# Four small experts in 64 slots, as plain fp32 matmuls in column pairs, in an order sorted on the chip

## The chip, the cores and the metric
The kernel runs on one core of a Trainium2 chip. Times are device microseconds of one launch, from the launch to the last instruction's end. The core's engines are PE (matmuls; PEld is its weight loads), DVE, ACT, POOL and SP, whose queue issues nearly all DMA transfers.

## What is computed
A two-layer trunk on 256 tokens of 1024 channels. The change lies in its last part, a mixture of experts: the router picks two of eight experts for a token, and an expert is a SwiGLU with 2816 hidden channels.

```
logits = xf @ router_w + router_b
top_vals, top_idx = lax.top_k(logits, 2)
gates = softmax(top_vals)
combine = sum(one_hot(top_idx, 8) * gates[..., None], axis=1)
for e in range(8):
    ye = (silu(xf @ w1[e]) * (xf @ w3[e])) @ w2[e]
    out = out + combine[:, e:e + 1] * ye
```

Ahead of it stand an RMSNorm, attention, pooling, a dense SwiGLU and a state-space mixer; behind it a residual and the final RMSNorm. All arrays are fp32.

## The kernel before
Only an expert's own tokens are computed. The router's logits become one-hots and ranks (a token's slot within its expert), and `Rows` (L1093) gathers the rows of an expert with matmuls of the tokens by a token-to-slot one-hot `P` of 128 slots. `scatter` (L1150) brings the outputs back with the transposed one-hot `PT`. Should an expert have over 128 tokens, a branch at the end (L1284) runs it again for the rest.

The weights are packed into tiles of 128 x 2048 fp32 (1 MB). An expert has 11 blocks (`NBLK`) of 256 hidden channels, and a block three tiles: two (A) of w1 beside w3, one (B) of w2. `load` (L87) takes a tile from a ring of 11 buffers (`raw`: 3 and `NR2` = 8) and issues its DMA on SP's queue. So the 264 tiles of the experts are issued in the order of use, each as soon as its buffer is free.

A product of fp32 values is made of three fp32r matmuls: `split` (L105) makes `hi` (a cast, ACT, L116) and `lo` (a subtraction, DVE, L117) of each half of a tile, in a ring of seven half tiles (`hi`: 6 and `NH2` = 1), and `mm3` (L120) multiplies hi by hi, hi by lo and lo by hi (L121 to L123). The rows are split likewise (`gx`, L1138 and L1140).

For each block `experts` (L1222) issues ffn_in (24 matmuls of 128 slots by 512 columns into a bank `p`), then ffn_out of the block before (12 matmuls into two banks `y`), then `ffn_T`: two transposes of the gated product `g` (Silu on ACT, L489, a multiply on DVE, L490), whose result is split into `th` and `tl` (L504). Two experts share one gather; experts run in the order 0 to 7. Engines run their own instructions in order. That order comes from a scheduler, which also moves instructions between the lines of the program.

Of the kernel before, what the change touches and what calls it, by code (L numbers as in the profile page):

```python
# [15 lines left out]
D = 1024  # L16
# [10 lines left out]
NR2, NH2 = 8, 1  # L27


# tiles of the packed weights, by number  # L30
# [6 lines left out]
def trunk_kernel(tc, x, par, cb, w_pool, wt, we, final_norm, out):  # L37
# [17 lines left out]
    with es:  # L55
# [38 lines left out]
        class Halves:  # L94
            """a tile of 2048 columns in two halves"""
# [29 lines left out]
        # -------------------------------------------------------- constants  # L125
# [3 lines left out]
        # small parameters: gains, forget bias, S5 scalars, forget and router weights  # L129
# [21 lines left out]
        def keep_clock(n, *behind):  # L151
            """short matmuls that keep the tensor engine's clock up over a wait"""
# [8 lines left out]
        def rms(src, junk):  # L161
            """returns 1 / rms, and the last instructions on ACT, DVE and Pool"""
# [44 lines left out]
        # S5 discretisation: a e^{dt} in polar form  # L207
# [23 lines left out]
        # ============================================================ mixer 0  # L231
        with ExitStack() as e0:
# [4 lines left out]
            # forget-gate selectors: row r = 32 i + h  # L237
# [14 lines left out]
            # causal mask of a diagonal block, four heads wide  # L252
# [6 lines left out]
            # 1 / min(t + 1, window)  # L259
# [12 lines left out]
            # ---- norm, transposed activations  # L272
# [14 lines left out]
            # ---- projections, channels on partitions  # L287
# [18 lines left out]
            # log sigmoid(z) = min(z, 0) - ln(1 + exp(-|z|))  # L306
# [24 lines left out]
            # ---- pooling branch  # L331
# [21 lines left out]
            # ---- q (scaled, one head per slot, the other head's rows zero), k, v  # L353
# [28 lines left out]
            # pooled map  # L382
# [15 lines left out]
            # ---- attention  # L398
# [125 lines left out]
        # ------------------------------------------------- complex helpers  # L524
# [63 lines left out]
                        # masks of the two groups of a pair, by state row and by channel row  # L588
# [14 lines left out]
                        # (abar - 1) / a  # L603
# [30 lines left out]
                        # e^{i 4 theta 2^k}  # L634
# [15 lines left out]
                            # Re(C a^tau) and -Im(C a^tau)  # L650
# [57 lines left out]
                    # chunk rotation e^{i 4 theta c}  # L708
# [69 lines left out]
        # ============================================================ mixer 1  # L778
# [80 lines left out]
        # ---- chunk inputs, chunk scan, outputs; four pairs at a time.  # L859
        # The gated projection of a block of channels follows its group.  # L860
# [68 lines left out]
        # ================================================================ MoE  # L929
# [25 lines left out]
        def route_T(tb, c0, n, i):  # L955
            """n blocks of 128 channels: sum of squares, transposed activations"""
# [71 lines left out]
        moe2 = pool("moe2", bufs=2)  # L1028
        gu[0] = pool("gu2")
# [28 lines left out]
        cmx = f6.tile([128, NE + 1], F32, name="cmx")  # L1058
        sc.copy(cmx[:, 0:NE], t[:, 16:24])
# [3 lines left out]
        cnts = rt.tile([128, NE + 1], I32, name="cnts")  # L1063

        def gates():
# [15 lines left out]
            ve.tensor_copy(cnts, cmx)  # L1081
# [283 lines left out]
```

## Time and profile before

| | us |
|---|---|
| runs | 1259.91, 1267.09, 1259.91 |
| median of the runs | 1259.91 |
| span of the profiled execution, first to last instruction | 1262.1 |
| PE busy in it | 1213.5 (96%) |
| DVE, ACT busy | 1084.0 (86%), 855.3 (68%) |

The runs' times do not say which of them was profiled; the span lies 2.2 above the median. Times in rows are us from the span's start, a mean or median of one instruction is in ns. A matmul's recorded duration overlaps with the next one's, so the distance of two starts, not the duration, says what a matmul costs.

### The profile page before, as it was taken

What the parts mean: (1) busy time and instruction counts of PE and PEld (TensorE: products, weight loads), DVE (VectorE), ACT (ScalarE), POOL (GpSimd) and SP (SyncE); (2) the same over time, 40 slices, a digit from 0 to 9 for tenths busy, and PEclk for the clock granted to TensorE, in tenths of its full rate; (3) what the DMA queues carried; (4) which work ended last, traced back from release to release, by engine and by line L of the source; (5) the groups of instructions that cost most, each with busy time, mean ns of one, the idle gap of its engine ahead of it and who ended that gap; (6) DMA issues with size and microseconds to landing.
All of it is one profiled execution on the core that took longest, in us unless ns stands there. A gap on an engine that the chain in (4) does not pass through costs nothing.

```text
span 1262.1 us, 16883 instructions
## 1 busy us (share of the span) xinstructions
PE 1213.5 (96%) x6188; PEld 998.6 (79%) x6189; DVE 1084.0 (86%) x1424; ACT 855.3 (68%) x1179; POOL 127.7 (10%) x132
## 2 busy tenths in 40 slices
PE   8998789999999999999999999999999999999995
PEld 8876568888878778888888888888888888888884
DVE  7776986688697779999999998899999999899996
ACT  6465336544475548888877877677777778777774
POOL 3303992000022110000000000000000000000000
PEclk9999789999999999999999999999999999999998
DMA  6524343543531658999998998998999997999960
GB/s 247 200 75 153 118 157 113 188 159 142 200 137 65 271 230 337 373 372 349 372 345 318 371 362 326 339 367 305 362 371 352 364 375 290 368 374 345 366 243 36
DMA packets 48138, 341.85 MB, mean 271 GB/s; under 512 B 5296, under 2 KB 5936, under 8 KB 6832
## 3 DMA queue, kind: packets, MB, share of 16 engines
q1 hardware_dynamic: 47904, 340.55, 71.7%
q8 instruction: 50, 0.82, 0.3%
q14 instruction: 40, 0.33, 0.1%
q10 hardware_dynamic: 144, 0.15, 0.0%
HBM read 339.63 MB, written 1.05 MB: 270 GB/s over the span
## 4 chain that ended last, share of the span: by engine, by line
PE 85%; DVE 9%; ACT 3%; issue 1%; POOL 1%; DMA 0%; ACTq 0%; DVEq 0%; POOLq 0%
PE p L122 16%; PE p L123 16%; PE p L121 15%; PE y L123 10%; PE y L121 10%; PE y L122 10%; DVE lo L117 3%; PE t L501 2%; PE t L1129 1%; PE t L687 1%; PE p L1129 1%; PE t L677 1%; ACT hi L116 1%; DVE ep L811 1%; PE t L874 0%
## 5 line engine op out<-in xcount | busy, mean ns | idle before, releaser
L117 DVE TENSOR_TENSOR lo<-raw,hi 128x1024 fp32r<-128x1024 f32 x642 | 777.1, 1244 | 91.1 <-ACT hi L116 77.1
L116 ACT CAST hi<-raw 128x1024 fp32r<-128x1024 f32 x642 | 650.0, 1050 | 123.1 <-PE y L123 46.7
L121 PE MATMUL p<-hi,gx 128*128 128x512 f32 x704 | 281.7, 401 | 0.0
L123 PE MATMUL p<-hi,gx 128*128 128x512 f32 x704 | 277.0, 393 | 0.0
L122 PE MATMUL p<-lo,gx 128*128 128x512 f32 x704 | 276.3, 393 | 0.0
L123 PE MATMUL y<-hi,tl 128*128 128x512 f32 x440 | 173.6, 395 | 3.1 <-DVE tl L504 3.1
L122 PE MATMUL y<-lo,th 128*128 128x512 f32 x440 | 172.8, 393 | 0.6 <-DVE lo L117 0.6
L121 PE MATMUL y<-hi,th 128*128 128x512 f32 x440 | 160.6, 393 | 0.2 <-ACT th L504 0.2
L122 PEld LDWEIGHTS p<-lo,gx 128*128 128x128 f32 x704 | 132.5, 188 | 30.0 <-DVE lo L117 1.1
L123 PEld LDWEIGHTS p<-hi,gx 128*128 128x128 f32 x704 | 132.2, 188 | 26.6
L121 PEld LDWEIGHTS p<-hi,gx 128*128 128x128 f32 x704 | 132.4, 188 | 25.4
L489 ACT ACTIVATE g<-p,rs 128x256 f32<-128x256 f32 x88 | 41.9, 476 | 86.7 <-PE p L123 86.6
L123 PEld LDWEIGHTS y<-hi,tl 128*128 128x128 f32 x440 | 83.1, 189 | 21.1 <-DVE tl L504 3.4
L122 PEld LDWEIGHTS y<-lo,th 128*128 128x128 f32 x440 | 82.9, 188 | 19.3 <-DVE lo L117 1.0
L121 PEld LDWEIGHTS y<-hi,th 128*128 128x128 f32 x440 | 83.1, 189 | 18.5 <-ACT th L504 0.5
L1187 POOL TENSOR_TENSOR fr<-fr,mhalf 128x1 f32<-128x1 f32 x2 | 1.5, 758 | 790.1 <-DVE fr L1185 790.1
L504 ACT CAST th<-t 128x256 fp32r<-128x256 f32 (+1 forms) x99 | 39.0, 394 | 56.3 <-PE t L501 56.3
L122 PE MATMUL p<-lo,h1h 128*128 128x512 f32 x176 | 71.6, 407 | 1.6 <-DVE lo L117 1.6
L121 PE MATMUL p<-hi,h1h 128*128 128x512 f32 x176 | 72.0, 410 | 0.0
L123 PE MATMUL p<-hi,h1l 128*128 128x512 f32 x176 | 70.8, 403 | 0.4 <-DVE h1l L204 0.4
L501 PE MATMUL t<-ident,g 128*128 128x128 f32 x220 | 41.1, 275 | 11.1 <-DVE g L490 11.1
L501 PEld LDWEIGHTS t<-ident,g 128*128 128x128 f32 x220 | 30.0, 141 | 25.3 <-DVE g L490 12.3
(382 smaller groups left out, 1455.8 us busy)
## 6 DMA issues: line engine op xcount, KB each, us to landing
raw<-in_we_dram SPq DMA_DIRECT2D x264, 1024.0 KB, 5.0
raw<-in_wt_dram SPq DMA_DIRECT2D x57, 1024.0 KB, 4.8
xt<-in_x_dram SPq DMA_DIRECT2D x2, 512.0 KB, 4.6
CB<-in_cb_dram SPq DMA_DIRECT2D x1, 1024.0 KB, 5.0
out_dram<-raw SPq DMA_DIRECT2D x4, 256.0 KB, 3.3
raw<-in_final_norm_dram SPq DMA_DIRECT2D x1, 512.0 KB, 4.2
wpl<-in_w_pool_dram SPq DMA_DIRECT2D x1, 256.0 KB, 9.1
pk<-in_par_dram ACTq DMA_DIRECT2D x1, 150.5 KB, 4.4
```

Source lines behind the costliest of these rows:

```text
L116: sc.copy(h.a[k][:, c], r[:, d])
L117: ve.tensor_sub(lo.a[k][:, c], r[:, d], f32(h.a[k][:, c]))
L121: pe.matmul(o, lh, rh, start=start, stop=False)
L122: pe.matmul(o, lh, rl, start=False, stop=False)
L123: pe.matmul(o, ll, rh, start=False, stop=stop)
L489: sc.activation(g1, p[:, 0:256], AF.Silu, scale=rs[:, tb:tb + 1])
L501: i0 = pe.transpose(v[:, f, tb * 128:(tb + 1) * 128], gs[tb][:, f * 128:(f + 1) * 128], ident)
L504: ffn_T.last = i0, sc.copy(th, v), ve.tensor_sub(tl, v, f32(th[:]))
L677: pe.transpose(t[:, k * 128:(k + 1) * 128], Vd[:, 2 * n2 + k // 2, k % 2].rearrange("p a b c -> p (a b c)"), ident)
L687: pe.matmul(t[0:32, k * 64:(k + 1) * 64], Bm[:, k, i].rearrange("p a b -> p (a b)"), Wu[:, c0 + k, i, 0:4].rearrange("p a b -> p (a b)"), ...
L811: ve.tensor_tensor_scan(ep[:, i], dv, ep[:, i], 0.0, op0=OP.mult, op1=OP.add)
L1129: pe.matmul(v, x_[:, tb, kc * 128:kc * 128 + 128], self.P[:, tb, 0:self.w], start=i + tb == 0, stop=i + tb == 2)
```

## The change
Expert 0 stays first, with 128 slots. Experts 1 to 7 are sorted by their number of tokens on the chip (`by_count`: 23 small DVE operations that also permute ranks and gates). The four with the fewest (positions 1 to 4, `NF` = 4) get 64 slots and take the new path; the other three stay as before. The order is 0, 1, 7, 2, 6, 3, 5, 4 by position, so large and small alternate. SP reads the expert's number into a register (`values_load`), and the DMA's address is made from it.

The new path does not split: `fast_in` multiplies 64 rows (stationary) by 256 columns of the raw tile in plain fp32, once for each half of the hidden channels, into the lower and the upper 64 partitions of one bank; `fast_out` does the same with the two halves of the output channels, 512 columns each. A branch still runs what does not fit into 64 or 128 slots. `raw` has 10 buffers instead of 11, `hi` six halves instead of seven. A large expert is gathered alone, all small ones together.

```diff
-NR2, NH2 = 8, 1
+NR2, NH2 = 7, 0
+NF = 4
...
+        order = [0]
+        for i in range(NE - 1):
+            order.append(i // 2 + 1 if i % 2 == 0 else NE - 1 - i // 2)
+
+        def room(p):
+            return 64 if 0 < p <= NF else 128
...
+        def by_count():
+            N = NE - 1
+            key = f6.tile([128, N], F32, name="key")
+            io1 = ioS[:, 1:NE]
+            ve.scalar_tensor_tensor(key, cmx[:, 1:NE], 8.0, io1, op0=OP.mult, op1=OP.add)
+            less = f6.tile([128, N, N], F32, name="less")
+            ve.tensor_tensor(less, key.unsqueeze(1).to_broadcast([128, N, N]),
+                             key.unsqueeze(2).to_broadcast([128, N, N]), op=OP.is_lt)
+            pos = f6.tile([128, N], F32, name="pos")
+            ve.tensor_reduce(pos, less, axis=AX.X, op=OP.add)
...
+            ve.tensor_copy(permi[:, 1:NE], num[:, 0, 1:NE])
+            for tb in range(2):
+                for s, d in ((rank[:, tb, 1:NE], rankp[:, tb, 1:NE]), (rg[:, tb, 2:], rgp[:, tb, 2:])):
+                    ve.tensor_tensor(tmp, sel, s.unsqueeze(1).to_broadcast([128, N, N]), op=OP.mult)
+                    ve.tensor_reduce(d, tmp, axis=AX.X, op=OP.add)
...
+        class Weights:
+            def __init__(self, p):
+                self.p = p
+                if p:
+                    self.r = nc.values_load(permi[0:1, p:p + 1], engines=[mybir.EngineType.SP], ...)
+            def load(self, i):
+                if self.p == 0:
+                    return load(we, i)
+                r = raw_tile()
+                nc.sync.dma_start(out=r, in_=we4[bass.ds(self.r, 1), i].rearrange("a p f -> (a p) f"))
+                return r
...
+        def fast_in(A, F, i):
+            p = ptile()
+            for s in range(2):
+                v = A[s].rearrange("p (k w f) -> p k w f", k=4, w=2)
+                for k in range(4):
+                    kc = 4 * s + k
+                    for h in range(2):
+                        pe.matmul(p[64 * h:64 * h + 64, 0:256].rearrange("p (w f) -> p w f", w=2),
+                                  F.x[:, kc, i * 64:i * 64 + 64], v[:, k, :, h * 128:h * 128 + 128],
+                                  start=kc == 0, stop=kc == 7)
+            g1 = gu[0].tile([128, 256], F32, name="g1", tag="g1")[:, 0:128]
+            sc.activation(g1, p[:, 0:128], AF.Silu, scale=F.rs[:, i, 0:1])
+            ve.scalar_tensor_tensor(g1, p[:, 128:256], F.rs[:, i, 1:2], g1, op0=OP.mult, op1=OP.mult)
+            return g1
+
+        def fast_T(g1):
+            t = ttile()
+            pe.transpose(t[:, 0:128], g1, ident)
+            h = gu[0].tile([128, 128], F32, name="hT", tag="hT", bufs=2)
+            sc.copy(h, t[:, 0:128])
+            return h
+
+        def fast_out(y, h, B, first, last):
+            for f in range(2):
+                for nb in range(2):
+                    c = f * D + nb * 512
+                    pe.matmul(y[64 * nb:64 * nb + 64], h[:, f * 64:f * 64 + 64], B[:, c:c + 512],
+                              start=first and f == 0, stop=last and f == 1)
...
+        def scatter_fast(P, y, acc, first, last):
+            t = ttile()
...
+            sc.copy(PT.rearrange("p a b -> p (a b)"), t[:, 0:256])
+            yf = tab.tile([128, 512], F32, name="yf", tag="t2")
+            sc.copy(yf[:, 0:256], y[:, 0:256])
+            ve.tensor_copy(yf[:, 256:512], y[:, 256:512])
+            o1 = [ttile(), ttile()]
+            for tb, os, i, j in ((0, acc, first, last), (1, o1, True, True)):
+                for nb in range(2):
+                    r = slice(64 * nb, 64 * nb + 64)
+                    pe.matmul(os[nb], PT[r, tb], yf[r], start=i, stop=j)
...
+                    gs = fast_in(A, F, p - 1) if fast else ffn_in(A, R.hi, R.lo, 1, R.rs[:, 0:1], R.rs[:, 1:2])
                     if prev is not None:
                         tail(prev)
                     if b == 0:
-                        ys = [[ytile(), ytile()]]
-                    prev = (e, b, *ffn_T(gs), ys, P)
...
+                        ys = [ytile()] if fast else [ytile(), ytile()]
+                    prev = (n, b, fast_T(gs) if fast else ffn_T(gs), ys, F if fast else R, W)
+                    if n == 0 and b == 1 and not off:
+                        by_count()
+                    if b == NBLK - 2 and n + 1 < len(todo):
+                        if room(todo[n + 1]) == 64:
+                            F = F or gathered_fast()
+                        else:
+                            nxt = gathered(Slow(todo[n + 1]))
...
-        experts(gather([0, 1], 0), [[2, 3], [4, 5], [6, 7]], 0)
+        R0 = Slow(0)
+        gates()
+        experts(order, gathered(R0))
```

How the instructions lie on the engines, at the places the prediction speaks of. The line numbers of the kernel after are its own: L118 and L119 are the split, L123 to L125 `mm3`, L1242 `fast_in`, L1252 `fast_T`, L1262 `fast_out`.

DVE at the start of the expert stage, before: `P` are the one-hots, `rg` the gates, `gx` the gathered rows, `lo` the splits.

```order
L1103 TENSOR_SCALAR P<-ioS,rank 128x128
L1078 SCALAR_TENSOR_TENSOR rg<-oh,gt,rg 128x8
L1081 CAST cnts<-cmx 128x9
L1103 TENSOR_SCALAR P<-ioS,rank 128x128
L1079 TENSOR_SCALAR rg<-rg,r_3906 128x8
L1103 TENSOR_SCALAR P<-ioS,rank 128x128 x2
L1140 SCALAR_TENSOR_TENSOR gx<-t,pk,gx 128x256 x2
L1140 SCALAR_TENSOR_TENSOR gx<-p,pk,gx 128x256 x2
L1140 SCALAR_TENSOR_TENSOR gx<-t,pk,gx 128x256 x2
L1140 SCALAR_TENSOR_TENSOR gx<-p,pk,gx 128x256 x2
L1115 COPY rs<-t 128x4
L117 TENSOR_TENSOR lo<-raw,hi 128x1024 x4
```

The same place after. `key` to `tmpp` belong to `by_count`.

```order
L1079 TENSOR_SCALAR rg<-oh,gt 128x8
L1104 SCALAR_TENSOR_TENSOR key<-cmx,ioS 128x7
L1124 COPY num<-cmx 128x1
L1080 SCALAR_TENSOR_TENSOR rg<-oh,gt,rg 128x8
L1106 TENSOR_TENSOR less<-key 128x49
L1081 TENSOR_SCALAR rg<-rg,r_3903 128x8
L1109 TENSOR_REDUCE pos<-less 128x7
L1128 TENSOR_SCALAR ov<-num 128x1
L1111 TENSOR_TENSOR selp<-ioS,pos 128x49
L1116 TENSOR_TENSOR tmpp<-selp,ioS 128x49
L1117 TENSOR_REDUCE num<-tmpp 128x7
L1116 TENSOR_TENSOR tmpp<-selp,cmx 128x49
```

Ahead of the first `gx` now stand the sorting and the eight one-hots `PF` of the small experts.

PE in a small expert after, blocks 7 and 8 of the first one: `x16` are the 16 matmuls of one fast_in.

```order
L1242 MATMUL p<-raw,xf 64x256 x16
L1262 MATMUL y<-raw,hT 64x512 x4
L1252 MATMUL t<-ident,g_5472 128x128
L1242 MATMUL p<-raw,xf 64x256 x16
L1252 MATMUL t<-ident,g_5506 128x128
L1262 MATMUL y<-raw,hT 64x512 x4
L1242 MATMUL p<-raw,xf 64x256 x16
L1252 MATMUL t<-ident,g_5540 128x128
L1262 MATMUL y<-raw,hT 64x512 x4
```

And before, around the transposes of a block: `y` is ffn_out, `p` the next ffn_in.

```order
L121 MATMUL y<-hi,th 128x512
L122 MATMUL y<-lo,th 128x512
L123 MATMUL y<-hi,tl 128x512
L501 MATMUL t<-ident,g_4774 128x128 x2
L121 MATMUL p<-hi,gx 128x512
L122 MATMUL p<-lo,gx 128x512
L123 MATMUL p<-hi,gx 128x512
```

The transpose of a block stood behind the ffn_out of the block before it; after, from block 7 of the first small expert and block 2 of the later ones, it stands ahead of it.

ACT at an expert's end before: `yhl` and `PT` belong to the scatter, `hi` to the splits.

```order
L489 ACTIVATE g_6969<-p,rs 128x256
L116 CAST hi<-raw 128x1024
L1159 CAST yhl<-y 128x512
L116 CAST hi<-raw 128x1024
L1155 CAST PT<-t 128x256
L1159 CAST yhl<-y 128x512
L116 CAST hi<-raw 128x1024 x2
L504 CAST th<-t 128x256
L116 CAST hi<-raw 128x1024 x3
L489 ACTIVATE g_7070<-p,rs 128x256
```

After, at the change from a large to a small expert: L491 is the large expert's last Silu, L1246 the small one's first, L118 the split of the large expert's last B tile.

```order
L506 CAST th<-t 128x256
L118 CAST hi<-raw 128x1024 x4
L491 ACTIVATE g_7833<-p,rs 128x256
L506 CAST th<-t 128x256
L1246 ACTIVATE g_7889<-p,rsf 128x128
L1274 CAST PT<-t 128x256
L118 CAST hi<-raw 128x1024 x2
L1278 CAST yhl<-y 128x512 x2
L1254 COPY hT<-t 128x128
L1246 ACTIVATE g_7962<-p,rsf 128x128
```

That split has moved behind the Silu of the next expert's first block and behind `PT`.

## Rows read from the trace of the kernel before

**Rows 1.** The page, part 4: the chain of work that ended last, shares of the span by engine and by line.
```profile
PE 85%; DVE 9%; ACT 3%; issue 1%; POOL 1%; DMA 0%; ACTq 0%; DVEq 0%; POOLq 0%
PE p L122 16%; PE p L123 16%; PE p L121 15%; PE y L123 10%; PE y L121 10%; PE y L122 10%; DVE lo L117 3%; PE t L501 2%; PE t L1129 1%; PE t L687 1%; PE p L1129 1%; PE t L677 1%; ACT hi L116 1%; DVE ep L811 1%; PE t L874 0%
```

**Rows 2.** Stretches of 100 us of the expert stage: length, then busy us (instructions) of PE, PEld, DVE, ACT and POOL, granted clock of PE, mean busy share of the DMA engines, GB/s.
```profile
500.00:600.00 100.00, 100.00 (x451) 81.61 (x450) 94.74 (x99) 81.15 (x96) 0.00 (x0) 1.00 0.96 365
...
700.00:800.00 100.00, 100.00 (x450) 81.62 (x450) 88.77 (x93) 75.33 (x92) 0.00 (x0) 1.00 0.92 351
800.00:900.00 100.00, 100.00 (x469) 82.34 (x468) 91.93 (x106) 76.22 (x100) 0.00 (x0) 1.00 0.89 338
```

**Rows 3.** Timeline of one block of an expert and of the ends of the blocks beside it: start, us, engine and line, operation, tiles, count, and in brackets the idle time before it and what ended that.
```profile
823.37 0.39 PE L123 MATMUL p<-hi,gx 128*128 128x512 f32 x1
823.60 0.62 PE L121 MATMUL y<-hi,th 128*128 128x512 f32 x2
...
823.80 0.48 ACT L489 ACTIVATE g<-p,rs 128x256 f32<-128x256 f32 x1 [1.33 <-PE p L123]
...
824.17 1.99 ACT L116 CAST hi<-raw 128x1024 fp32r<-128x1024 f32 x2
...
825.24 2.36 DVE L117 TENSOR_TENSOR lo<-raw,hi 128x1024 fp32r<-128x1024 f32 x2 [0.45 <-ACT hi L116]
...
825.89 0.39 PE L122 MATMUL y<-lo,th 128*128 128x512 f32 x1
...
826.12 0.40 PE L123 MATMUL y<-hi,tl 128*128 128x512 f32 x1
...
826.36 0.38 PE L501 MATMUL t<-ident,g 128*128 128x128 f32 x2
...
832.29 0.47 ACT L489 ACTIVATE g<-p,rs 128x256 f32<-128x256 f32 x1 [1.35 <-PE p L123]
```

**Rows 4.** Timeline of PE: the first matmul of the expert stage, and its last ffn_out matmul with the scatter behind it.
```profile
470.68 0.48 PE L121 MATMUL p<-hi,gx 128*128 128x512 f32 x1
...
1246.85 0.40 PE L123 MATMUL y<-hi,tl 128*128 128x512 f32 x1
...
1247.09 0.42 PE L1162 MATMUL y<-yhl,PT 128*128 128x512 f32 x1
```

**Rows 5.** What SP's queue waited for between 450 and 1230 us (us in total, times, longest); the transfers of expert weights (KB each, median us from issue to landing); and the stretch of 25 us in which the ring of tiles was filled, with the columns of rows 2.
```profile
SPq L89 <- DVE lo L117: 520.4, 205, 17.1
SPq L89 <- DVE tl L504: 146.6, 44, 5.1
...
raw<-in_we_dram SPq DMA_DIRECT2D x264, 1024.0 KB, 5.0
...
425.00:450.00 25.00, 24.30 (x119) 19.70 (x118) 15.31 (x30) 14.86 (x21) 0.23 (x1) 1.00 1.01 427
```

**Rows 6.** Plain fp32 matmuls elsewhere in the kernel, from PE's timeline: the pooled map (L387) and, between two `mm3`, the state inputs (L796); then, of one line each, the durations in ns (least, median, greatest) and the first and last start.
```profile
67.09 1.89 PE L387 MATMUL t<-pl,wpl 128*128 128x256 f32 x8
...
358.69 0.40 PE L123 MATMUL y<-hi,h2l 128*128 128x512 f32 x1
359.02 1.15 PE L796 MATMUL p<-um,W 128*64 128x64 f32 x32
360.10 0.51 PE L121 MATMUL y<-hi,h2h 128*128 128x512 f32 x1
...
L387 PE MATMUL t<-pl,wpl x8: 378/379/379, 67.1 to 68.6; 128*128 128x256 f32 x8
...
L796 PE MATMUL p<-um,W x256: 222/222/270, 359.0 to 412.6; 128*64 128x64 f32 x128
```

**Rows 7.** Groups of instructions by line and shape: count, busy us, mean ns of one, idle before. The first two are a scaled copy and a multiply from a bank at 128x128, the others belong to the scatter.
```profile
L201 ACT ACTIVATE h1h<-t,pk 128x128 fp32r<-128x128 f32 x16 | 4.4, 377 | 6.2 <-PE t L189 6.2
...
L204 DVE SCALAR_TENSOR_TENSOR h1l<-t,pk,h1h 128x128 fp32r<-128x128 f32 x16 | 4.4, 344 | 2.2 <-ACT h1h L201 2.2
...
L1166 DVE TENSOR_TENSOR xt<-xt,t 128x512 f32<-128x512 f32 x14 | 9.4, 680 | 1.4 <-PE t L1163 1.4
...
L1155 ACT CAST PT<-t 128x256 fp32r<-128x256 f32 x7 | 2.6, 371 | 0.3
```

**Rows 8.** Timeline of the start of the expert stage (one-hots, small operations on the gates, the gather and its results on DVE), and the stretch of 5 us behind it.
```profile
463.67 0.87 DVE L1103 TENSOR_SCALAR P<-ioS,rank 128x128 fp32r<-128x128 f32 x4
...
464.45 0.23 DVE L1079 TENSOR_SCALAR rg<-rg,r 128x8 f32<-128x8 f32 x1
...
464.72 0.15 DVE L1080 TENSOR_REDUCE cmx<-cmx 128x1 f32<-128x8 f32 x1
...
467.33 0.87 DVE L1140 SCALAR_TENSOR_TENSOR gx<-t,pk,gx 128x256 fp32r<-128x256 f32 x2 [1.33 <-ACT gx L1138]
...
468.69 0.40 PE L1129 MATMUL t<-P,xl 128*128 128x256 f32 x2
...
468.93 0.40 PE L1129 MATMUL p<-P,xh 128*128 128x256 f32 x2
...
469.86 0.95 PE L1112 MATMUL t<-rg,P 128*128 128x2 f32 x8
...
470.00:475.00 5.00, 5.00 (x28) 4.25 (x27) 4.46 (x8) 3.88 (x5) 0.00 (x0) 1.00 0.00 0
```

**Rows 9.** Timeline of PE behind a long wait in the dense SwiGLU.
```profile
153.67 0.90 PE L501 MATMUL t<-ident,g 128*128 128x128 f32 x3 [7.61 <-DVE g L490]
154.23 0.78 PE L121 MATMUL p<-hi,h1h 128*128 128x512 f32 x1
154.80 0.63 PE L122 MATMUL p<-lo,h1h 128*128 128x512 f32 x1
155.23 0.63 PE L123 MATMUL p<-hi,h1l 128*128 128x512 f32 x1
...
157.76 0.40 PE L123 MATMUL p<-hi,h1l 128*128 128x512 f32 x1
157.99 0.40 PE L121 MATMUL p<-hi,h1h 128*128 128x512 f32 x1
```

More of the change, by code (lines that the diff above doesn't have):

```diff
@@ L1028, in trunk_kernel @@
         moe2 = pool("moe2", bufs=2)
+        fastp = pool("fastp")
         gu[0] = pool("gu2")
@@ L1150, in scatter, with scale @@
-        def scatter(e, P, ys, acc, first, last):
+                for kc, gcl, v in gather_mm(t, self.P[:, :, :, 0], NF * 64, range(2 * j, 2 * j + 2)):
+                    if j % 2:
+                        ve.tensor_scalar(self.x[:, kc], v, gcl, None, op0=OP.mult)
+                    else:
+                        sc.activation(self.x[:, kc], v, AF.Copy, scale=gcl)
+            def scale(self, t):
+                for i in range(NF):
+                    for tb in range(2):
+                        pe.matmul(t[:, 2 * i:2 * i + 2], f32(self.P[:, tb, i]).rearrange("p a b -> p (a b)"),
+                                  rgp[:, tb, 0:3 + i:2 + i], start=tb == 0, stop=tb == 1)
+                ve.tensor_copy(self.rs, t[:, 0:2 * NF].rearrange("p (a b) -> p a b", a=NF))
@@ L1151, in scatter, with to_tokens @@
+        def to_tokens(o, tb, nb, last):
+            xo = xt[:, tb, nb * 512:nb * 512 + 512]
+            ve.tensor_add(xo, xo, o)
+        def scatter(P, ys, acc, first, last):
             t = ttile()
@@ L1211, in final, with gathered, gathered_fast @@
             return norm
-        def gather(es, g):
-            R = Rows(es, g)
-            if not g:
-                gates()
-            for j in range(4):
-                R.bank(j, (ttile, ptile)[j % 2]())
+        def gathered(R):
+            for j in range(2):
+                R.mm(j, (ttile, ptile)[j]())
+            R.evac()
+            R.evac()
             R.scale(ttile())
             return R
-        def experts(R, rest, g):
-            gate = {} if g else {(0, 1): R.last}
-            elist = R.es + sum(rest, [])
+        def gathered_fast():
+            F = Fast()
+            for j in range(4):
+                F.bank(j, (ttile, ptile)[j % 2]())
+            F.scale(ttile())
+            return F
@@ L1226, in experts @@
+        def experts(todo, R, off=0):
+            gate = {} if off else {(0, 1): R.last}
             acc = [ytile(), ytile()]
+            F = None
+            prev = None
             def tail(st, B=None):
-                e, b, th, tl, ys, P = st
-                last = b == NBLK - 1
-                with after(*gate.get((e, b + 1), ())):
-                    B = B or split(load(we, (e * NBLK + b) * 3 + 2))
-                ffn_out(ys, th, tl, B, b == 0, last)
-                if last:
-                    scatter(e, P, ys, acc, e == elist[0], e == elist[-1])
@@ L1237, in experts @@
-            prev = None
-            ys = None
-            for e in elist:
-                P, rh, rl, rs = R.of(e)
-                N = None
-                more = rest if e == R.es[-1] else []
-                for b in range(NBLK):
-                    A = [split(load(we, (e * NBLK + b) * 3))]
-                    with after(*gate.get((e, b), ())):
-                        A.append(split(load(we, (e * NBLK + b) * 3 + 1)))
-                    if b == NBLK - 1 and more:
-                        N = Rows(more[0], g)
-                        rest = rest[1:]
-                        N.mm(0, ttile())
-                        N.mm(1, ttile())
-                    gs = ffn_in(A, rh, rl, 1, rs[:, 0:1], rs[:, 1:2])
-                    if N:
-                        N.evac()
-                        N.evac()
+                n, b, h, ys, R, W = st
@@ new lines, in tail @@
+                p = todo[n]
+                first, last = n == 0, n == len(todo) - 1
+                end = b == NBLK - 1
+                fast = room(p) == 64 and not off
+                if B is None:
+                    B = W.load(b * 3 + 2)
+                if fast:
+                    fast_out(ys[0], h, B, b == 0, end)
+                    if end:
+                        scatter_fast(R.P[:, :, p - 1], ys[0], acc, first, last)
+                else:
+                    if not isinstance(B, tuple):
+                        with after(*gate.get((n, b + 1), ())):
+                            B = split(B)
+                    ffn_out([ys], *h, B, b == 0, end)
+                    if end:
+                        scatter(R.P, ys, acc, first, last)
@@ new lines, in experts @@
+            for n, p in enumerate(todo):
+                fast = room(p) == 64 and not off
+                W = Weights(p) if fast else R.w
+                nxt = None
+                for b in range(NBLK):
+                    A = [W.load(b * 3)]
+                    if not fast:
+                        A[0] = split(A[0])
+                    A.append(W.load(b * 3 + 1))
+                    if not fast:
+                        with after(*gate.get((n, b), ())):
+                            A[1] = split(A[1])
+                    gs = fast_in(A, F, p - 1) if fast else ffn_in(A, R.hi, R.lo, 1, R.rs[:, 0:1], R.rs[:, 1:2])
@@ L1275, in experts @@
                 norm()
-        experts(gather([0, 1], 0), [[2, 3], [4, 5], [6, 7]], 0)
+        R0 = Slow(0)
+        gates()
+        experts(order, gathered(R0))
         def count(i):
-            return nc.values_load(cnts[0:1, i:i + 1], min_val=0, max_val=T,
-                                  skip_runtime_bounds_check_because="a count of T tokens")
-        with tc.If(count(NE) > 128):
-            for e in range(NE):
-                with tc.If(count(e) > 128):
-                    experts(gather([e], 1), [], 1)
+            return nc.values_load(over[0:1, i:i + 1], min_val=0, max_val=T,
+                                  skip_runtime_bounds_check_because="a count of T tokens at most")
+        with tc.If(count(NE) > 0):
+            for p in order:
+                with tc.If(count(p) > 0):
+                    experts([p], gathered(Slow(p, room(p))), room(p))
             final()()
```

138 lines of the change are left out of this document (80 added, 58 removed).

## Prediction, before the changed kernel was run
> **What bounds the kernel now.** I read the chain of waits first: it is PE for 85% of the span, and six of its lines, the three matmuls of `mm3` in ffn_in and in ffn_out, make up 77% [rows 1]. The stretches of 100 us come next. From 500 us on PE has no idle time, at a granted clock of 1.00 (2.4 GHz), DVE is 89 to 95% busy, ACT 75 to 81%, and the DMA engines move 338 to 365 GB/s [rows 2]. Three resources look nearly full, so the third view asks who waits for whom. In one block ACT's `g` starts at 823.80 and again at 832.29, so a block takes 8.49 us, which is 36 matmuls 0.229 us apart (0.23 in the rows) and two transposes. PE goes from ffn_in to ffn_out to the transposes without a gap, while ACT waits 1.33 us for PE [rows 3]. The expert stage runs from the first ffn_in at 470.68 to the last ffn_out matmul at 1247.25, 776.6 us: 88 blocks of 8.49 are 747.1, and gathers and scatters take the other 29.5 [rows 4]. The DMA queue waits 520.4 us for `lo` (the splits that free a weight tile) and 146.6 us in the group named `tl`, and a tile lands 5.0 us after its issue. Its rate is therefore set by the consumer. When eleven free tiles were filled, it ran at 427 GB/s with PE and DVE at work [rows 5]. So PE bounds this stage, and DMA could give a 1.0486 MB tile every 2.45 us against the 2.83 that are used.
>
> **The part that gets shorter.** A small expert's block has 16 matmuls of 64 output rows by 256 columns and 4 of 64 by 512, all plain fp32 on the unsplit tile. The trace has both ingredients. At L387 four fp32 matmuls of 256 columns stand as eight PE instructions, 1.89 us in all, the last 0.379: (1.89 - 0.38)/7 = 0.216 us each. At L796 32 instructions with 64 stationary columns, writing the upper and lower half of a bank in turn, take 1.15 us, the last 0.222: 0.030 us each, where 64/256 of 0.216 would be 0.054 [rows 6]. So the two halves overlap almost wholly. I take two instructions per 0.216 us: 16 pairs are 3.45 us for ffn_in, and 4 pairs of twice the columns 1.72 us for ffn_out. The `order` rows of one small block also show a 128-wide transpose between them. Going into and out of the half-width matmuls costs about 0.1 us each: L796 starts 0.33 us after the last L123 matmul, where 0.23 is usual [rows 3, 6]. With 0.11 for the transpose and two such changes a block is 5.47 us. The Trainium skill (TensorEngine Tiling (Array Packing), Tiling Modes) says that changing the tiling mode drains the engine. The 0.1 us agrees with that; if it were free, 44 blocks would be 9 us shorter.
>
> **The sum for the stage, from 470.68 to the last ffn_out.**
> Large experts: 44 blocks of 8.49 are 373.6. They keep the splits, and the splits keep the place shown in the rows; six half tiles instead of seven still hold the three tiles of a block. A stall for one would cost at most 1.0 us a block (one cast, 1.05 [rows 3]); I take none.
> Small experts: 44 blocks of 5.47 are 240.7.
> Waits for the transpose: in 26 or 27 of the 44 blocks the program has the transpose right behind ffn_in, ahead of ffn_out. PE then stands until Silu (0.377 at 128x128), the multiply (0.344) and three hand-overs are through; with the 0.16 us that a matmul's record outlasts its streaming this is 0.95 us [rows 3, 7]. 26.5 of them are 25 us (15 to 30).
> Gathers: the one of all small experts has 32 matmuls of 256 columns at 0.117 and eight short fp32 ones, 4.5 us, beside the first expert. Three gathers of a large expert have 128 columns in fp32r, which the trace lacks. Between half of 0.117 and the 0.22 of two fp32 instructions of 128 columns, 32 are 1.9 to 7.0 us; I take 4, nearer the first row. Together 16.5 (10 to 25) [rows 6, 8].
> Scatters of large experts: eight matmuls and two transposes, 2.05 us, 8.2 for four. In three of them the program now has the small expert's first ffn_in ahead of the last ffn_out, and the split of that last tile behind ffn_in's Silu on ACT. PE waits for Silu, copy, cast and subtraction (0.38 + 0.37 + 1.05 + 1.24 and hand-overs, less what it can begin), and after the scatter for a bank that DVE's additions (0.68 each) free: 4.3 us each, 14.4 in all with 1.5 for the first (0 to 24) [rows 3, 7].
> Scatters of small experts: four fp32 matmuls of 512 columns on 64 rows each. If the row halves overlap as the column halves do they take 1.7 us, else 3.4; 2.75 with the transposes, three in the stage, 8.2 (6 to 11).
> From small to large: the casts of the large expert's first tiles stand behind `PT` on ACT, so PE waits for two copies, a cast and a subtraction, some 3 us, and about 1 us more before the next block: 4 each, 12 for three (6 to 18) [rows 3, 7].
> Start: the sorting (23 small DVE operations, 0.15 to 0.23 us each by their neighbours) and eight one-hots (0.2 apart) now stand between the first one-hots and the first `gx` on DVE. That takes DVE from about 464.1 to 471 us, where `gx` began at 467.33 and ffn_in, held by a gather of twice the width, at 470.68. I take 2 us (0 to 6) [rows 4, 8].
> The sum is 373.6 + 240.7 + 25 + 16.5 + 22.6 + 8.2 + 12 + 2 = 700.6 us against 776.6: 76.0 gained, with both ends of every term 40 to 110. The last scatter has one more narrow step than before, 1 us, so the span is 1262.1 - 75.0 = 1187. The run times are 1259.91, 1267.09, 1259.91, and none is marked as the profiled one; the median stands 2.2 us under the span, so I forecast 1185 us.
>
> **Whether the weights keep up.** By 475 us the ring stands full (0 GB/s in 470:475) [rows 8], so ten of the 264 tiles are there and 254 have to come. At 2.45 us these need 622 us, until 1097, well before the stage ends. Within a small expert 33 tiles go in about 77 us while 31 arrive, and some seven lie ready from the large expert before. The expert numbers reach the DMA queue by one register load per expert; it waits on DVE's sorting of the first microseconds and is issued ten tiles ahead.
>
> **Rivals.**
> DMA becomes the bound (0.13). The stage's best 100 us, 365 GB/s [rows 2], is what has been sustained; 427 was seen for 25 us. At 2.87 us a tile 254 tiles end at 1204; the last ffn_out (1.7), the ending (14.9) and the extra 1 us, 17.6 together, give 1222, as a run 1219. Against it: in the expert stage the queue waited for buffers [rows 5].
> The Trainium skill (DMA: Bandwidth & Descriptors, Where 436 GB/s comes from) goes further: for loads from HBM the memory side, about 358 GB/s per core, binds. The rows disagree with 427 [rows 5], but only for 25 us. That rule would make the same rival end at 475 + 254 x 2.93 + 17.6, as a run 1234; I give it 0.05.
> The clock falls at the changes of expert (0.06). After 7.61 us without work matmuls came 0.43 us apart from 154.23 to about 157.8, then 0.23 [rows 9], some 2 us lost. Waits of 3 to 4 us at seven changes would add 14: 1199. Against it: PE's other waits here are about 1 us.
> The pairs do not overlap when the moving side is 256 or 512 columns wide (0.06). A small block then is 32 x 0.216 + 8 x 0.43 + 0.3 = 10.66 us, 5.19 more, 228 in all: 1413, slower. It decides once a small block exceeds 5.47 + 75/44 = 7.17 us, that is with less than two thirds of the overlap. For it: nothing in the trace pairs wide instructions for long; against it: L796.
> The change does not do what it says if one of the four smallest has over 64 tokens: a branch then runs that expert again, over 100 us, 1295 (0.01). The router of the reference on these inputs gives experts 1 to 7 57, 125, 58, 49, 95, 41, 30 tokens, so the fourth smallest has 57.
>
> **How the numbers follow.** The forecast's own case has 0.62, its range by the bounds of its terms is 1150 to 1220, and 0.07 is left for waits beyond them. I reach up to the second DMA rival: 1150 to 1234. A measurement of this kernel can tell about 1% from no change, 1247 to 1272. Faster takes all cases but the serial pairs and the rerun, with part of the remainder: 0.89; within 1% 0.03, slower 0.08.
>
> **What would show it.** A small block should repeat every 5.5 us without and 6.4 with the wait for the transpose, large blocks every 8.49; the instructions of fast_in should start in pairs 0.216 us apart; DMA should exceed 400 GB/s in small experts with PE's waits going to DVE or ACT. PE waiting for `raw` in most blocks would mean that DMA binds; half-width instructions 0.2 us apart one by one would make the prediction wrong.

## The result, and the profile after

The changed kernel takes 1205.35 us (median of 1203.25, 1206.46, 1204.23 and 1207.35), the one before 1260.98 in the runs beside it: a ratio of 0.9556, interval 0.9529 to 0.9583. The forecast was 1185, with a range of 1150 to 1234. The profiled execution has a span of 1201.4 us and is the run of 1203.25; a run is 1.7 to 1.9 us longer than its span in all that follows. So 60.7 us of span went, where 75 were forecast.

Stretches of 50 us in the expert stage of the changed kernel, with the columns of [rows 2]: a large expert, and three that lie mostly in small ones.

```profile
500.00:550.00 50.00, 50.00 (x224) 40.67 (x224) 46.95 (x48) 40.55 (x47) 0.00 (x0) 1.00 0.95 369
600.00:650.00 50.00, 45.85 (x309) 26.96 (x306) 8.96 (x19) 10.29 (x26) 0.00 (x0) 0.97 1.01 426
750.00:800.00 50.00, 44.87 (x302) 23.84 (x302) 5.34 (x12) 5.87 (x17) 0.00 (x0) 0.97 0.91 374
950.00:1000.00 50.00, 44.61 (x329) 24.82 (x327) 3.55 (x12) 6.61 (x22) 0.00 (x0) 1.00 1.01 426
```

In a large expert PE is as full as in [rows 2], with DVE, ACT and DMA at nearly the same rates. In a small one DVE falls to between 7 and 18% and ACT to between 12 and 21%, PE has some 10% of idle time that it did not have before, and DMA moves 426 GB/s in two of the three stretches.

PE's timeline in two places of the changed kernel: in the first small expert, where a block's transpose (L1252) stands behind ffn_out (L1262), and in the third one, where it stands ahead of it.

```profile
589.28 0.33 PE L1252 MATMUL t<-ident,g 128*128 128x128 f32 x1
589.54 3.67 PE L1242 MATMUL p<-raw,xf 128*64 128x256 f32 x32
593.04 1.89 PE L1262 MATMUL y<-raw,hT 128*64 128x512 f32 x8
594.86 0.33 PE L1252 MATMUL t<-ident,g 128*128 128x128 f32 x1
...
966.64 0.33 PE L1252 MATMUL t<-ident,g 128*128 128x128 f32 x1 [0.85 <-DVE g L1247]
966.90 1.94 PE L1262 MATMUL y<-raw,hT 128*64 128x512 f32 x8
968.66 3.62 PE L1242 MATMUL p<-raw,xf 128*64 128x256 f32 x32
973.14 0.33 PE L1252 MATMUL t<-ident,g 128*128 128x128 f32 x1 [0.85 <-DVE g L1247]
```

A block repeats after 5.58 us in the first place and after 6.50 in the second, where PE waits 0.85 us for `g`. The 32 instructions of fast_in take 3.50 us, 0.216 us for every two: the halves overlap, as the prediction took from L796.

What PE and SP's queue waited for in the changed kernel between 460 and 1200 us (PE) and 450 and 1200 us (SP): us in total, times, longest.

```profile
PE t L1252 <- DVE g L1247: 22.2, 28, 0.9
PE p L123 <- ACT hi L118: 4.2, 3, 1.4
PE y L123 <- ACT hi L118: 4.2, 3, 1.4
...
SPq L1147 <- DVE lo L119: 188.1, 81, 8.3
SPq L1147 <- PE p L1242: 143.0, 79, 7.4
...
SPq L1147 <- DMA raw<-in_we_dram: 1.6, 3, 0.7
```

PE never waits for a weight tile, and the queue still waits for buffers [rows 5]. Nearly all the waits of PE that are left are the transposes and the first tiles at the changes of expert. One such change, from a large expert to a small one, in the timeline of the changed kernel:

```profile
745.95 0.44 PE L1273 MATMUL t<-ident,P 128*128 128x128 f32 x2
746.06 0.37 ACT L1246 ACTIVATE g<-p,rsf 128x128 f32<-128x128 f32 x1 [3.24 <-PE p L1242]
746.42 0.37 ACT L1274 CAST PT<-t 128x256 fp32r<-128x256 f32 x1
...
746.69 1.99 ACT L118 CAST hi<-raw 128x1024 fp32r<-128x1024 f32 x2
...
747.79 0.74 PE L123 MATMUL y<-hi,th 128*128 128x512 f32 x2 [1.41 <-ACT hi L118]
...
749.05 0.50 PE L124 MATMUL y<-lo,th 128*128 128x512 f32 x1 [0.52 <-DVE lo L119]
...
750.26 0.63 PE L125 MATMUL y<-hi,tl 128*128 128x512 f32 x1
```

ACT stood idle for 3.24 us in front of the small expert's Silu, with the casts of the large expert's last tile queued behind it; PE then waits for these casts. From 750 us on the matmuls come 0.43 us apart instead of 0.23. The granted clock shows why (stretches of 3 us, changed kernel):

```profile
744.00:747.00 3.00, 2.38 (x22) 1.25 (x18) 0.58 (x3) 0.94 (x3) 0.00 (x0) 1.00 0.57 180
747.00:750.00 3.00, 1.69 (x6) 1.12 (x7) 2.40 (x3) 1.68 (x2) 0.00 (x0) 0.97 1.01 385
750.00:753.00 3.00, 3.00 (x9) 1.86 (x7) 0.31 (x2) 0.58 (x1) 0.00 (x0) 0.50 0.94 339
```

PE was busy for 4.07 of 6 us, and then ran at 0.50 (1.2 GHz). This happens at four of the seven changes, from about 644, 750, 931 and 1112 us, for 3.4 us each.

### The profile page after: what moved, and what is told of

Same layout as the page of the kernel before. It is cut to its first block, busy times and chain, and to the rows that moved or that the text cites. A ratio compares the mean times of both kernels' runs of the same rounds, so it can differ in the third digit from the quotient of the medians.

```text
span 1201.4 us, 16867 instructions
## 1 busy us (share of the span) xinstructions
PE 1116.3 (93%) x6353; PEld 831.5 (69%) x6353; DVE 752.7 (63%) x1139; ACT 583.2 (49%) x915; POOL 130.1 (11%) x132
## 4 chain that ended last, share of the span: by engine, by line
PE 81%; DVE 12%; ACT 3%; issue 2%; POOL 1%; DMA 0%; ACTq 0%; DVEq 0%; POOLq 0%
PE p L1242 13%; PE p L125 10%; PE p L124 10%; PE p L123 9%; PE y L125 8%; PE y L124 8%; PE y L123 7%; PE y L1262 7%; DVE lo L119 4%; PE t L503 1%; PE t L1252 1%; ACT g L1246 1%; ACT hi L118 1%; PE t L1168 1%; DVE g L1247 1%
## 5 line engine op out<-in xcount | busy, mean ns | idle before, releaser
L119 DVE TENSOR_TENSOR lo<-raw,hi 128x1024 fp32r<-128x1024 f32 x378 | 463.9, 1262 | 85.1 <-ACT hi L118 78.6
L118 ACT CAST hi<-raw 128x1024 fp32r<-128x1024 f32 x378 | 381.7, 1050 | 104.5 <-PE y L125 49.2
L1242 PE MATMUL p<-raw,xf 128*64 128x256 f32 x1408 | 164.8, 381 | 0.0
L123 PE MATMUL p<-hi,gx 128*128 128x512 f32 x352 | 143.6, 408 | 4.2 <-ACT hi L118 4.2
L1242 PEld LDWEIGHTS p<-raw,xf 128*64 128x64 f32 x1408 | 99.9, 137 | 63.0 <-issue 17.4
L124 PE MATMUL p<-lo,gx 128*128 128x512 f32 x352 | 139.3, 396 | 3.7 <-DVE lo L119 3.7
L125 PE MATMUL p<-hi,gx 128*128 128x512 f32 x352 | 139.6, 396 | 0.0
L124 PE MATMUL y<-lo,th 128*128 128x512 f32 x264 | 106.8, 405 | 3.6 <-DVE lo L119 3.6
L125 PE MATMUL y<-hi,tl 128*128 128x512 f32 x264 | 107.0, 405 | 2.1 <-DVE tl L506 2.1
L1246 ACT ACTIVATE g<-p,rsf 128x128 f32<-128x128 f32 x44 | 16.1, 367 | 185.1 <-PE p L1242 185.1
L123 PE MATMUL y<-hi,th 128*128 128x512 f32 x264 | 98.8, 402 | 4.2 <-ACT hi L118 4.2
L1262 PE MATMUL y<-raw,hT 128*64 128x512 f32 x352 | 86.1, 601 | 0.0
L123 PEld LDWEIGHTS p<-hi,gx 128*128 128x128 f32 x352 | 67.0, 190 | 22.0 <-ACT hi L118 7.4
L125 PEld LDWEIGHTS p<-hi,gx 128*128 128x128 f32 x352 | 66.8, 190 | 13.9
L123 PE MATMUL p<-hi,h1h 128*128 128x512 f32 x176 | 71.9, 410 | 0.0
L125 PE MATMUL p<-hi,h1l 128*128 128x512 f32 x176 | 71.0, 403 | 0.4 <-DVE h1l L206 0.4
L124 PEld LDWEIGHTS y<-lo,th 128*128 128x128 f32 x264 | 50.8, 193 | 17.3 <-DVE lo L119 5.3
L123 PEld LDWEIGHTS y<-hi,th 128*128 128x128 f32 x264 | 50.2, 191 | 16.5 <-ACT hi L118 4.9
```

Source lines behind the costliest of these rows:

```text
L118: sc.copy(h.a[k][:, c], r[:, d])
L119: ve.tensor_sub(lo.a[k][:, c], r[:, d], f32(h.a[k][:, c]))
L123: pe.matmul(o, lh, rh, start=start, stop=False)
L124: pe.matmul(o, lh, rl, start=False, stop=False)
L125: pe.matmul(o, ll, rh, start=False, stop=stop)
L1242: pe.matmul(p[64 * h:64 * h + 64, 0:256].rearrange("p (w f) -> p w f", w=2), F.x[:, kc, i * 64:i * 64 + 64], v[:, k, :, h * 128:h * 128 + ...
```

## The experiments

The seven runs were made in two groups, and the kernel before took 1263.89 us beside the first group (the first four below) and 1262.41 beside the second, against 1260.98 beside the changed kernel. Differences between groups are therefore good to some 3 us; smaller ones are read from the traces. In the edits `with after(x)` has what follows issued behind the instruction `x`, each on its own engine.

**The transpose behind ffn_out.**

```
-                    pe.matmul(y[64 * nb:64 * nb + 64], ...)
+                    fast_out.last = pe.matmul(y[64 * nb:64 * nb + 64], ...)
...
-                    prev = (n, b, fast_T(gs) if fast else ffn_T(gs), ...)
+                    with after(*((fast_out.last,) if fast and b else ())):
+                        hT = fast_T(gs) if fast else ffn_T(gs)
+                    prev = (n, b, hT, ...)
```

> In small experts the transpose of a block is queued behind the ffn_out of the block before it; nothing else is changed. Theory A (a wait for the hand-over Silu, multiply): after it all blocks of small experts repeat every 5.58 us as the first ones do, where 24 blocks took 6.50; 24 x 0.92 = 22 us go, time about 1183, and PE's wait for g at the transposes falls from 22 us to nearly 0. Theory B (DMA is what really limits small experts): they then need 33 tiles in about 68 us instead of 73; at 365 GB/s 24 arrive and some 7 lie ready, so PE would wait for raw some 6 us in each of four experts, time about 1203 to 1206.

Measured: 1179.50 us (ratio 0.9338, 0.9316 to 0.936), 25.9 less than the changed kernel. PE's timeline in its third small expert:

```profile
950.45 1.89 PE L1262 MATMUL y<-raw,hT 128*64 128x512 f32 x8
952.27 0.33 PE L1252 MATMUL t<-ident,g 128*128 128x128 f32 x1
952.52 3.67 PE L1242 MATMUL p<-raw,xf 128*64 128x256 f32 x32
```

The waits for `g` are gone and PE's waits for `raw` sum to 1.4 us: theory A. Some 3 us more went at the changes of expert, and these tell the clock's price apart. Here is the same change as above in this kernel, where it lies at 738 to 750 us:

```profile
741.00:744.00 3.00, 1.59 (x15) 0.75 (x11) 0.84 (x4) 1.81 (x4) 0.00 (x0) 1.00 0.92 339
744.00:747.00 3.00, 2.48 (x10) 1.72 (x11) 2.26 (x2) 0.81 (x1) 0.00 (x0) 1.00 0.75 243
747.00:750.00 3.00, 3.00 (x13) 1.91 (x12) 1.53 (x3) 1.07 (x2) 0.00 (x0) 1.00 0.98 366
```

PE is as idle as before (4.07 of 6 us busy), with the same waits, but the clock stays at 1.00. What a change costs over plain blocks (from the start of the small expert's first ffn_in to that of its third, less two ffn_in of 3.50, a large ffn_out of 2.80, a small one of 1.82 and two transposes of 0.26 us) is 5.7 us here and 7.24 in the changed kernel: a fall of the clock costs 1.5 us. In this kernel the clock falls at two other changes instead, from a small to a large expert (at 814.6 and 988.7 us), which cost 1.6 us more than the same changes of the changed kernel, where it did not fall. Two falls instead of four are the 3 us. What decides at which changes the clock falls was not found.

**The casts first at the changes.**

```
...
+                    BB, cast = None, ()
+                    if fast and b == 0 and room(todo[n - 1]) == 128:
+                        BB = split(prev[5].load((NBLK - 1) * 3 + 2))
+                        cast = (split.last,)
+                    with after(*cast):
+                        gs = fast_in(A, F, p - 1) if fast else ffn_in(...)
...
+                    if fast and b == NBLK - 1 and nxt is not None:
+                        A0 = split(nxt.w.load(0))
+                        cast2 = (split.last,)
+                    with after(*cast2):
+                        hT = fast_T(gs) if fast else ffn_T(gs)
```

> At a change from a large to a small expert the last B tile of the large one is loaded and split ahead of the small one's first Silu; at a change from a small to a large one the first A tile of the large one is cast ahead of the copies hT and PT. Arithmetic is the same. Theory A (the order on ACT makes PE wait at the changes, and the waits make the clock fall): large to small goes from 7.24 us over the plain blocks to 3.1, as at the change from expert 0, small to large from 6.7 to 8.3 down to about 4; the half-speed stretches of 3.4 us are gone; 3 x 4.1 + 3 x 3 = 21 us less, about 1184. Theory B (the clock falls at a change in any case, since PE does little in it): only the waits themselves go, about 10 us, 1195, and stretches at a granted clock of 0.50 remain at the six changes. Theory C (PE waits for the tiles themselves): no change, 1205.

Measured: 1187.36 us (ratio 0.939, 0.9371 to 0.9409), 18.0 less. The two kinds of change in its timeline:

```profile
644.78 0.38 PE L1290 MATMUL t<-ident,PF 128*128 128x128 f32 x2
644.92 0.48 PE L123 MATMUL p<-hi,gx 128*128 128x512 f32 x1
645.16 0.27 ACT L1254 COPY hT<-t 128x128 f32<-128x128 f32 x1
...
645.63 0.51 PE L124 MATMUL p<-lo,gx 128*128 128x512 f32 x1 [0.23 <-DVE lo L119]
...
746.17 0.37 ACT L1246 ACTIVATE g<-p,rsf 128x128 f32<-128x128 f32 x1 [1.35 <-PE p L1242]
746.24 0.71 PE L123 MATMUL y<-hi,th 128*128 128x512 f32 x2
...
746.53 0.48 DVE L1181 TENSOR_SCALAR P<-ioS,rankp 128x128 fp32r<-128x128 f32 x2 [3.15 <-PE t L1273]
...
748.20 0.51 PE L124 MATMUL y<-lo,th 128*128 128x512 f32 x1 [1.24 <-DVE lo L119]
```

From small to large the first matmul follows the transposes at once, and such a change, measured in the same way, falls from 6.75 us (8.3 for the one at which the clock fell) to 4.5. From large to small the waits for the casts are gone; at the first of the three the subtraction still stood behind a one-hot on DVE that waited 3.15 us for PE, and this change took 4.8 us, the other two 3.3, where 7.24 were paid. The clock is at 1.00 at all seven changes. The sum of the changes is 10.4 + 8.2 = 18.6 us less, of which the four falls of the clock are about 6: theory A for the waits. That the waits alone make the clock fall, as theory A has it, is not shown: in the run before this one it stayed up at three changes with the same waits. PE did not wait for the tiles.

**Without the 64-slot path.** `NF = 4` becomes `NF = 0`.

> NF = 0: the sorting, the order by count, the register for the DMA's address and the smaller rings stay, but all eight experts run with 128 slots in three split matmuls. Theory A (the whole gain is the unsplit path): 88 blocks of 8.5, seven gathers of one expert at 4.9 us in place of three of two, so 10 to 20 us slower than the kernel before: 1270 to 1282. Theory B (part of the gain comes from the ring, the order or the dynamic addresses): under 1255.

Measured: 1278.24 us in a single run, theory A. Its stretches are those of [rows 2]:

```profile
500.00:600.00 100.00, 100.00 (x468) 82.36 (x467) 93.23 (x105) 79.89 (x101) 0.00 (x0) 1.00 0.91 350
```

So what is left of the change without the path (the sorting, the single gathers, the smaller rings, addresses from a register) costs together about 14 us over the kernel before in the same group, and the path gives back 73. A large expert's gather there makes its block 12.50 us instead of 8.47: 4.0, the value that the prediction took.

**The same matmuls one half after the other.**

```
-            for s in range(2):
-                ...
-                for k in range(4):
-                    kc = 4 * s + k
-                    for h in range(2):
+            for h in range(2):
+                for s in range(2):
+                    ...
+                    for k in range(4):
...
-            for f in range(2):
-                for nb in range(2):
+            for nb in range(2):
+                for f in range(2):
```

> The same instructions of fast_in and fast_out in another order: first all matmuls that write partitions 0 to 63, then all that write 64 to 127, so that neighbours no longer lie in different columns. Theory A (two column halves run at once only as neighbours in the queue): a pair's 0.216 us is paid twice, 16 x 0.216 + 4 x 0.43 = 5.2 us more in each of 44 blocks, about 228 us: 1430. Theory B (the overlap comes from elsewhere, or 64 columns are simply faster): 1205 to 1250.

Measured: 1314.26 us in a single run, 109 more than the changed kernel: between the theories. That is also 50 more than the kernel before, so without the alternation of the halves the change would have been a loss. The count of fast_in's instructions at work in stretches of 1.8 us of one block, those begun earlier included (columns: length, busy PE, busy PEld, clock, DMA share, GB/s):

```profile
606.60:608.40 1.80, 1.80 (x9) 1.17 (x10) 1.00 0.85 291
608.40:610.20 1.80, 1.80 (x14) 1.28 (x13) 1.00 1.00 410
610.20:612.00 1.80, 1.80 (x11) 1.17 (x9) 1.00 0.98 414
```

And PE's timeline of that block:

```profile
606.60 5.67 PE L1242 MATMUL p<-raw,xf 128*64 128x256 f32 x29
611.89 0.64 PE L1262 MATMUL y<-raw,hT 128*64 128x512 f32 x1
612.10 0.59 PE L1242 MATMUL p<-raw,xf 128*64 128x256 f32 x2
612.37 0.59 PE L1262 MATMUL y<-raw,hT 128*64 128x512 f32 x1
612.53 0.38 PE L1242 MATMUL p<-raw,xf 128*64 128x256 f32 x1
612.75 1.88 PE L1262 MATMUL y<-raw,hT 128*64 128x512 f32 x6
```

Nine are at work in the first stretch, where only one half has work in reach (0.216 us from start to start, as with 128 columns [rows 6]: 64 columns are not faster in themselves), and 14 in the next, where the end of one half meets the beginning of the other; the changed kernel has 18 in the first 1.8 us of a block and as many in the rest. An ffn_out of the lower half starts at 611.89 while three ffn_in of the upper half, which stand ahead of it in PE's queue, have yet to start. A matmul of fast_in stands as two instructions (32 for 16), so a queue in the order of the rows would break off after 29 and 31 in the middle of a matmul; the order of the queue does not explain that. So each half proceeds by itself, and PE looks about three instructions ahead for one of the idle half. A block takes 8.22 us, 2.64 more and not 5.2; 44 of them are 116 us, and the span grew by 111. PE waits for `g` as in the changed kernel (21.9 us), but the clock falls at one change instead of four, which gives some 4.5 us back. The Trainium skill (TensorE: Matmul & The Clock Gate, Part 3: Packing small matmuls) says that matmuls start and end strictly in the order of the queue; these rows show that between column halves they do not. Nor does PE here run its instructions strictly in order, as the part on the kernel before has it of all engines.

**Both edits together**, the transposes behind ffn_out and the casts first.

> The transposes behind ffn_out and the casts first at the changes, together. Theory A (separate costs, PE still the bound): the two gains add, 25.9 + 18.0 us, about 1161; a pair of a large and a small expert then takes PE about 167 us and DMA 66 tiles of 2.46 us, 162. Theory B (DMA is now the bound, since its stretches at 426 GB/s already last through a small expert and most of the next large one): PE waits for raw in the last blocks of small experts, 3 to 6 us in each of three, 1170 to 1180.

Measured: 1164.37 us (ratio 0.9226, 0.921 to 0.9241), 41.0 less than the changed kernel. PE's waits for `raw` are 1.8 us, so PE is still the bound: theory A. It is 3 us short of the sum because both edits had removed the same two falls of the clock: waits for `g` 22.2, changes 10.4 + 8.2, together 40.8.

**A fifth small expert**, on top of both edits.

```
-NF = 4
+NF = 5
...
-                for kc, gcl, v in gather_mm(t, self.P[:, :, :, 0], NF * 64, range(2 * j, 2 * j + 2)):
+                for kc, gcl, v in gather_mm(t, self.P[:, :, :, 0], NF * 64, range(j, j + 1)):
...
-        order = [0]
-        ...
+        order = [0, 1, 2, 7, 3, 4, 6, 5]
```

> The kernel 'both' with NF = 5: the expert with 58 tokens takes the 64-slot path too (its gather in eight banks of one column block), in the order large, small, small, large, small, small, large, small. PE alone would save 11 blocks of 8.53 - 5.58 and some changes, about 40 us: 1120. Theory A (DMA gives a 1.05 MB tile every 2.46 us and no more): two small experts in a row use 66 tiles in 135 us while 55 arrive and 7 lie ready; some 12 tiles of 2.46 us are missing in all, 29 us, so about 1148, with PE waiting for raw. Theory B (DMA is not at its limit at 427 GB/s): 1120 to 1130.

Measured: 1155.91 us (ratio 0.9151, 0.9134 to 0.9168), the fastest of all. What its PE waited for between 460 and 1200 us, what SP's queue waited for most, and a stretch of its second pair of small experts:

```profile
PE p L1240 <- DMA raw<-in_we_dram: 11.3, 33, 0.5
PE y L1260 <- DMA raw<-in_we_dram: 11.1, 19, 0.8
```

```profile
SPq L1145 <- DMA raw<-in_we_dram: 188.3, 109, 2.1
```

```profile
900.00:950.00 50.00, 43.25 (x303) 22.04 (x301) 2.45 (x7) 4.42 (x14) 0.00 (x0) 1.00 1.01 427
```

A block of the pair begins to repeat after 7.37 us instead of 5.58: three tiles of 2.46 us. The queue, which waited 1.6 us for transfers under way in the changed kernel, waits 188.3 here. DMA has become the bound, and 8.5 us are left of the 40 that PE was estimated to save: theory A, 8 us dearer than expected. PE's waits for tiles account for 22.4 of the 31.5 us that did not come; the other 9 were not assigned.

**The small experts last**: in the changed kernel `order = [0, 5, 6, 7, 1, 2, 3, 4]`.

> The changed kernel with another order only: the four large experts first, then the four small ones. Six of seven changes between large and small go, about 25 us of PE's time. Theory A (DMA is the bound once small experts stand together): from about 866 us on 122 tiles of 2.46 us are missing, 300 us, so the stage ends near 1169 and the run near 1190, with PE waiting for raw at 427 GB/s. Theory B (DMA keeps up): 1178 to 1180. Theory C (the changes cost nothing net): 1205.

Measured: 1199.86 us in a single run, between A and C; with 0.5% it is too near the changed kernel to be called faster. One of its stretches:

```profile
1050.00:1100.00 50.00, 40.70 (x273) 19.67 (x273) 2.29 (x7) 4.35 (x14) 0.00 (x0) 1.00 1.01 426
```

DMA moves 426 to 427 GB/s from 900 us to the end of the stage, its queue waits 149.1 us for transfers under way, and most of the later small blocks take 7.3 to 7.4 us: DMA binds, as A says. A's time was 10 us too low: it had DMA at its full rate from 866 us on, but while tiles lie ready the queue waits for PE to free a buffer, and from 850 to 900 us DMA moved only 298 GB/s, six tiles or 15 us fewer by estimate.

## Why the prediction was right, and where 20 us went

Each mechanism of the sum was there, and one that the forecast had put aside, the clock at the changes, came on top; the sizes, from the first ffn_in of before (470.68) to the last ffn_out:

| term | predicted | measured | from |
|---|---|---|---|
| large blocks | 373.6 | 375.3 | 44 x 8.53 |
| small blocks | 240.7 | 245.5 | 44 x 5.58 |
| waits for the transpose | 25 | 22.2 | PE's waits |
| gathers | 16.5 | 20.6 | 5.9 and 3 x 4.9 |
| large to small, with the scatter | 22.6 | 24.8 | 3.1 and 3 x 7.24 |
| small to large, with the scatter | 20.2 | 21.8 | 8.3 and 2 x 6.75 |
| start | 2 | 1.0 | below |
| not assigned | | 2.2 | |
| sum | 700.6 | 713.4 | |

- **The small block**, the term that missed by most, was 0.11 us short (4.8 us in 44 blocks): the changes to and from the half-width matmuls were priced at 0.1 each, 0.2 in all, and the rows of after show 0.3: 1.82 us from ffn_out to the transpose, where four pairs are 1.72, 0.26 from it to the next fast_in, where 0.11 was taken, and 3.50 for fast_in, where 16 pairs are 3.45.
- **The large block** grew by 0.04 to 0.06 us: ffn_out's matmuls come 0.233 us apart instead of 0.229 [rows 3]. With no small expert in the program they come at 0.229, so the six half tiles are not the cause; what is stays open.
- **The gathers** of large experts were sized right at 4.0 where they stand among 128-wide matmuls (`NF = 0`, small experts last), though by luck in part: with `NF = 0` the 32 matmuls of 128 columns of such a gather take 3.6 us (553.94 to 557.55), 0.112 each, hardly less than the 0.117 of 256 columns [rows 8]. They cost 0.9 more here because the program puts them in pieces among half-width matmuls, and each border costs 0.1 to 0.2. The gather of the small experts took 5.9 us instead of 4.5: its eight short fp32 matmuls stand as 16 instructions and take 1.7.
- **The rival of the clock** was written off too early. It was tied to waits of 3 to 4 us without work; the waits were 1.4 us, and it fell all the same, at four changes of seven, 1.5 us each, 6 us. That lies in the two rows of the changes: without it they would be some 2 us below the forecast, so that they came near is luck in part.
- **The start**: the sorting was hidden, but by a slow gather. PE ran at 0.50 for all of the stretch below, where the kernel before had 0.90 (first row after, second before). ffn_in began at 470.20, not later than before, and lost 1.5 us to the clock in its first block. So the term came near its 2 us for another reason than the one forecast. Why the clock stayed low for 17 us was not tried; it did so with `NF = 0` too, so it does not take the 64-slot path.

```profile
456.40:473.40 17.00, 16.55 (x71) 15.13 (x72) 12.90 (x75) 4.31 (x14) 1.79 (x2) 0.50 0.23 76
```

```profile
456.40:473.40 17.00, 14.38 (x95) 12.86 (x95) 13.81 (x59) 8.52 (x19) 1.84 (x3) 0.90 0.27 101
```

- **The tail** from the last ffn_out to the end is 17.3 us where 14.9 stood before; 1 us more was forecast, 2.4 came.
- **The step that was wrong in kind** is the one from span to time. The prediction took the median of before, 2.2 us under the span, as the offset. Every run here whose span is known is 1.7 to 1.9 us over it, so the profiled execution of before was one of about 1264, and the forecast span of 1187 meant 1189. So the 20 us are 12.8 of the stage, 1.4 of the tail, 4 of this offset, and 2 by which the median lies above the profiled run.
- **The range**: as listed, the bounds of the terms add up to a gain of 40 to 117 us, not 40 to 110, so its lower end would be 1143. Nothing hangs on it.
- **DMA**: the first rival (365 GB/s) and the second, by the page of the Trainium skill that the prediction names (358), were wrong: 426 GB/s over 50 us here, and over 250 us in the run with the small experts last. The Trainium skill has the other number as well (HBM Reference, Specifications (TRN2)): a core that streams alone measures about 425 GB/s. The rows agree with that page.

## What to carry to other kernels

When a stage's matmuls shrink, read the queue of every engine at the places where the old and the new kind of work meet: a cast behind a Silu cost PE 1.4 us and, at some of these places, the clock, and putting the casts first at six changes gave 18 us, as much as a quarter of the whole change's forecast. Where a dependent chain of 0.9 us stands in each block, put a block's independent matmuls between its ends (here 22 us). Then look which resource is next: at 427 GB/s DMA is 2.46 us a tile, and the fifth small expert gained a fifth of what PE alone was estimated to gain.

## What the runs showed of the hardware

- Two column halves of PE hold separate streams: a pair of fp32 instructions of 64 stationary and 256 moving columns starts 6 to 8 ns apart and takes 0.216 us, and with the halves one after the other PE still overlaps them over a few instructions (8.22 us a block against 5.58, where 10.8 was expected).
- The granted clock fell after PE had been busy for 4.07 of 6 us in one run and stayed at 1.00 after the same work in another; where it fell at a change of expert, it was 0.50 for 3.4 us and cost 1.5 us.
- A gather matmul of 128 columns in fp32r costs 0.112 us (with `NF = 0`), one of 256 columns 0.117 [rows 8].
- DMA held 426 to 427 GB/s for 250 us, with PE 81 to 87% busy.
